# A row-wise nanmax on one core: eighteen trial operations at the start, and one load cut into nine parts by partitions and columns

## The chip, the cores and the metric

The kernel runs on one core of one Trainium2 chip. Its time is device microseconds for one launch. Times of a kernel are given as the median of its timed runs; a profile is one further execution of the same program with the hardware profiler on.

## What is computed

```python
def setup_inputs():
    batch, seq, dim = 32, 2048, 2048
    x = np.random.randn(batch, seq, dim).astype(np.float32)
    mask = np.random.rand(batch, seq, dim) < 0.1
    x[mask] = np.nan
    return {"x": x, "axis": -1}

def reference(x, axis):
    return np.nanmax(x, axis=axis).astype(np.float32)
```

65,536 rows of 2,048 floats are read (537 MB), and one maximum per row is written (0.26 MB). A tenth of the numbers are NaN, and they must not win.

## The kernel before

**Tiles.** The rows are cut into 74 tiles, listed by hand in `TILES` and gathered in six groups. The unit of the list is a quarter of a row (Q = 512 elements). The first tile is one row for each of the 128 partitions (128 x 2048); nearly all others are seven rows (128 x 14336, 7168 KB). Towards the end the tiles have the same size or less, but their loads, pieces and reductions get smaller. An entry such as `([28], [7, 9, 12], [16, 12])` says: one load of 28 quarters; three pieces of 7, 9 and 12 quarters (128 x 3584, 128 x 4608 and 128 x 6144) that are cleaned one after the other; and two reductions of 16 and 12 quarters (four rows and three rows).

**What is done with a tile.** SyncE (SP) issues the load into one of three buffers `xt0`, `xt1`, `xt2` (tile number n goes to buffer (n-1) mod 3). ScalarE (ACT) then reads the upper 16 bits of each number, with a step of two 16-bit elements, and writes a contiguous 16-bit key into one of three key buffers `kt` (through `act`, line 226 of the profile). GpSimd (POOL) turns the key back (times -1, plus a constant) and writes it over the upper half of the number, again with a step of two (through `pool`, line 236): this is the "write-back", after which a NaN counts as a very low number. A minus sign in a tile's list of pieces gives that write-back to ACT instead (`release`, also line 226). VectorE (DVE) then takes the maximum along each row with a `tensor_reduce` (line 243). At the end the rows that held nothing but NaN are mended (lines 249 and 263) and the results are stored (line 455).

**What sets the order.** All of it stands in one critical section, and the class `Order` keeps the books: each engine's instructions run in the order in which they were added, every instruction raises its engine's semaphore, and `add` puts waits in front of an instruction for those dependences that its engine has not yet seen. Loads are issued on SP at line 307, in order. Each waits for `before`, the last reduction of the tile that used the buffer three tiles ago, and for `lanes[turn]`, the load that used the same one of 14 load semaphores before it. `free[...]` holds what the next user of a buffer waits for. A key operation waits for those loads of its tile that overlap its columns (`here`), and for the write-backs that still read the key buffer.

**What the change touches.** The block of loads (line 307 and the loop around it), the setup just before the loop over tiles (after line 269), and the end of a tile's turn, where `free` is set. Tile number 30 is an ordinary one, with the entry quoted above, in buffer `xt2`.

Of the kernel before, what the change touches and what calls it, by code (L numbers as in the profile page):

```python
# [8 lines left out]
D = 2048  # L9
# [53 lines left out]
LEAD = 128  # L63

LANES = 14

# [104 lines left out]
def kernel(  # L173
# [15 lines left out]
    nc = tc.nc  # L189
    P = nc.NUM_PARTITIONS  # L190
    f32, i32 = mybir.dt.float32, mybir.dt.int32
    i16, u16 = mybir.dt.int16, mybir.dt.uint16
    ALU = mybir.AluOpType
    ACT = mybir.ActivationFunctionType
# [7 lines left out]
    of = out.bitcast(i32).flatten_outer_dims().rearrange("r c -> (r c)")  # L202
# [10 lines left out]
    xts = [sing.tile([P, WIDE * D], i32, name=f"xt{i}") for i in range(BUFS)]  # L213
# [5 lines left out]
    with tc.tile_critical():  # L219
        order = Order(nc)  # L220

        def act(deps, pair=None, **kw):
            return order.add(
                "act",
                nc.scalar,
                lambda: nc.scalar.activation(**kw),  # L226
                deps,
                lane=pair,
                joint=pair is not None,
            )  # L230

        def pool(deps, pair=None, **kw):
            return order.add(
                "pool",
                nc.gpsimd,
                lambda: nc.gpsimd.tensor_scalar(**kw),  # L236
                deps,
                lane=pair,
                joint=pair is not None,
            )  # L240

        def dve(deps, do, **kw):
            return order.add("dve", nc.vector, lambda: do(**kw), deps)  # L243

        def find(who, engine, deps, acc, none, op):
            e = order.add(
                who,
                engine,
                lambda: engine.tensor_scalar(  # L249
                    out=none,  # L250
                    in0=acc,
                    scalar1=NONE,
                    scalar2=float(0x00800000),
                    op0=ALU.is_equal,
                    op1=ALU.mult,
                ),
                deps,
            )
            bits = acc.bitcast(i32)
            return order.add(  # L260
                who,
                engine,
                lambda: engine.tensor_tensor(  # L263
                    out=bits, in0=bits, in1=none, op=op
                ),
                [e],
            )

        e_top = order.add("dve", nc.vector, lambda: nc.vector.memset(top, EDGE), [])  # L269
        act([e_top], out=warm, in_=top, func=ACT.Prelu, alpha=0.5)  # L270

        free = [[] for _ in range(BUFS)]
        kfree = [[] for _ in range(NKEYS)]
        clock = 0
# [7 lines left out]
        number = 0  # L282
        lanes = [[] for _ in range(LANES)]
        turn = 0
# [4 lines left out]
        for gi, (s, g) in enumerate(zip(rows, GROUPS)):  # L289
            xg = xr[r0 : r0 + P * s].rearrange("(p s) d -> p (s d)", p=P)  # L290
# [4 lines left out]
            base = 0  # L295
            for loads, pieces, reds in g:
                assert sum(loads) == total(pieces) == sum(reds)
                xt, before = xts[number % BUFS], free[number % BUFS]
                number += 1
                landed = []  # L300
                at = 0
                for c in loads:
                    c *= Q
                    e = order.add(
                        "sp",
                        nc.sync,
                        lambda: nc.sync.dma_start(  # L307
                            out=xt[:, at : at + c], in_=xg[:, base + at : base + at + c]
                        ),
                        before + lanes[turn],  # L310
                        lane=f"load{turn}",
                        step=16,
                    )
                    lanes[turn] = [e]
                    turn = (turn + 1) % LANES
                    landed.append((at, at + c, e))
                    at += c
                clean = []
                after = []
                at = done = 0  # L320
# [7 lines left out]
                half = {}  # L328
# [16 lines left out]
                def name(i):  # L345
                    return f"pair{number}_{pairs[i][0]}" if i in pairs else None
# [15 lines left out]
                for parts in pieces:  # L362
                    parts = parts if isinstance(parts, tuple) else (parts,)
                    c = int(sum(map(abs, parts))) * Q
                    here = [l for a, b, l in landed if a < at + c and b > at]
                    kold = []
                    if used + c > KEYS:
# [9 lines left out]
                        out=kts[key][:, used : used + c],  # L377
                        in_=xt[:, at : at + c].bitcast(i16)[:, 1::2],
                        func=ACT.Prelu,
                        bias=top,  # L380
                        scale=-1.0,
# [3 lines left out]
                    for c in parts:  # L385
                        back, wait, c = c < 0, isinstance(c, float), int(abs(c)) * Q
                        kp = kts[key][:, used : used + c]
                        used += c
                        to = xt[:, at : at + c].bitcast(i16)[:, 1::2]
# [5 lines left out]
                        else:  # L395
                            e = pool(
                                [e_key],
                                name(piece),
                                out=to,
                                in0=kp,  # L400
                                scalar1=-1.0,
                                scalar2=float(TOP),
                                op0=ALU.mult,
                                op1=ALU.add,
# [4 lines left out]
                        while reds and done + reds[0] <= min([at] + open_):  # L409
                            n = reds.pop(0)  # L410
# [5 lines left out]
                            if done % D:  # L416
                                m, to = 1, xt[:, done - 1 : done].bitcast(f32)
                            else:
                                m = max(n // D, 1)
                                to = acc[:, row : row + m]  # L420
                            e = dve(
                                [e for a, b, e in clean if b > lo and a < done] + part,
                                nc.vector.tensor_reduce,
                                out=to,
                                in_=xt[:, lo:done]
                                .bitcast(f32)
                                .rearrange("p (c d) -> p c d", c=m),
                                axis=mybir.AxisListType.X,
                                op=ALU.max,
                            )  # L430
                            part = [e] if done % D else []
                            after.append(e)
                free[(number - 1) % BUFS] = after[-1:]
                base += at
            stores.append((og, acc.bitcast(i32)))
            if gi == LATE:
# [6 lines left out]
            else:  # L443
                e = find(
                    "dve", nc.vector, after, accs[:, lo:flagged], nones[:, lo:flagged], ALU.bitwise_or
                )
                ready += [e] * (gi + 1 - len(ready))
            if gi == len(GROUPS) - 1:
                e = find("pool", nc.gpsimd, late_after, late_acc, late, ALU.add)
                ready[LATE] = e  # L450
        for (og, bits), e in zip(stores, ready):
# [5 lines left out]
                lane="store",  # L457
                step=16,
# [39 lines left out]
```

## Time and profile before

| | us |
|---|---|
| median of 2 runs | 1252.91 (1252.86 and 1252.96) |
| span of the profiled execution, first to last instruction | 1251.3 |
| what lies around the span, median less span | 1.6 |
| POOL busy | 1169.5 (93%) |
| DVE busy | 1110.9 (89%) |
| ACT busy | 986.8 (79%) |

The profiled execution has no separate device time beside its span, so 1251.3 us plus the 1.6 us around it stand for it. Line numbers with an L are lines of the kernel before; "SPq" is SP's queue of DMA issues; "xt<-kt" names output and input. In the timeline the first number is the start in us, the second the time from the first to the last of the merged instructions, and what stands in brackets is the idle time before it and what ended it. In the table by form, "busy us, mean ns" are followed by the engine's idle time before such instructions.

### The profile page before, as it was taken

To read this page: it belongs to the slowest core of one execution; us is meant where nothing else is said; L and a number is where in the kernel's file an instruction comes from. 1 tells how busy PE (TensorE), PEld (TensorE's weight loads), DVE (VectorE), ACT (ScalarE), POOL (GpSimd) and SP (SyncE) were. 2 spreads that over 40 slices of the span, in tenths; PEclk is the share of its full clock that TensorE was granted. 3 is DMA by queue.
4 is the path that set the end of the run, shared out by engine and by line. 5 is a ranking of instruction groups with operands and counts; after the bars stand their busy time and mean duration, and the time that the engine had idled before them with its cause. 6 is when DMAs were issued, how large, how long until landed. Compare 5 with 4: busy or idle time off the path is not lost.

```text
span 1251.3 us, 893 instructions
## 1 busy us (share of the span) xinstructions
DVE 1110.9 (89%) x181; ACT 986.8 (79%) x273; POOL 1169.5 (93%) x242
## 2 busy tenths in 40 slices
DVE  0888989888889888898988888998888899999999
ACT  3777887778787877788777878777777878999998
POOL 2999989998999899998999899999999999989998
DMA  9999999999999999999999999999999999999997
GB/s 415 440 412 438 440 440 438 413 440 440 440 434 416 440 440 438 434 418 440 440 438 434 418 440 440 438 434 418 440 440 437 437 418 437 436 429 431 428 429 294
DMA packets 15991, 537.20 MB, mean 429 GB/s; under 512 B 2544, under 2 KB 2544, under 8 KB 3568
## 3 DMA queue, kind: packets, MB, share of 16 engines
q1 hardware_dynamic: 15984, 537.14, 99.3%
q14 instruction: 7, 0.06, 0.0%
HBM read 536.87 MB, written 0.26 MB: 429 GB/s over the span
## 4 chain that ended last, share of the span: by engine, by line
DMA 38%; DVE 27%; POOL 20%; ACT 13%; issue 1%; SPq 0%; ACTq 0%
DMA xt<-in_x_dram 38%; DVE acc L243 27%; POOL xt L236 20%; ACT kt L226 11%; ACT xt L226 2%; SPq L307 0%; DVE none L249 0%; DVE acc L263 0%; SPq L493 0%; ACTq L158 0%; SPq L219 0%
## 5 line engine op out<-in xcount | busy, mean ns | idle before, releaser
L236 POOL TENSOR_SCALAR xt<-kt 128x3584 int16<-128x3584 uint16 (+11 forms) x236 | 1168.4, 4951 | 77.0 <-ACT kt L226 59.2
L243 DVE TENSOR_REDUCE acc<-xt 128x3 f32<-128x6144 f32 (+4 forms) x175 | 1107.6, 6380 | 136.7 <-POOL xt L236 128.8
L226 ACT ACTIVATE kt<-xt,scalars 128x3584 uint16<-128x3584 int16 (+9 forms) x247 | 935.5, 3826 | 257.4 <-DMA xt<-in_x_dram 241.1
L226 ACT ACTIVATE xt<-kt 128x512 int16<-128x512 uint16 (+6 forms) x24 | 52.8, 2202 | 0.7
L226 ACT ACT_TABLE_LOAD x1 | 1.3, 1283 | 0.9 <-SPq L219 0.9
L243 DVE TENSOR_REDUCE xt<-xt 128x1 f32<-128x1536 f32 x1 | 1.7, 1742 | 0.0
L269 DVE MEMSET scalars<- 128x1 f32 x1 | 0.1, 59 | 1.0 <-SPq L219 1.0
L249 DVE TENSOR_SCALAR none<-acc 128x414 int32<-128x414 f32 (+1 forms) x2 | 0.8, 381 | 0.1
L263 DVE TENSOR_TENSOR acc<-acc,none 128x414 int32<-128x414 int32 (+1 forms) x2 | 0.8, 375 | 0.1
L249 POOL TENSOR_SCALAR late<-acc 128x91 int32<-128x91 f32 x1 | 0.5, 547 | 0.1
L263 POOL TENSOR_TENSOR acc<-acc,late 128x91 int32<-128x91 int32 x1 | 0.3, 339 | 0.1
L479 POOL MEMSET const-float32-0.0<- 128x1 f32 x1 | 0.1, 99 | 0.2 <-issue 0.2
L226 ACT ACTIVATE scalars<-scalars 128x1 f32<-128x1 f32 x1 | 0.2, 202 | 0.0
L479 POOL MEMSET const-uint8-127<- 128x1 uint8 x1 | 0.1, 103 | 0.0
L479 POOL MEMSET const-bfloat16-1.0<- 128x1 bf16 x1 | 0.1, 102 | 0.0
L479 POOL MEMSET const-float32-1.0<- 128x1 f32 x1 | 0.1, 99 | 0.0
## 6 DMA issues: line engine op xcount, KB each, us to landing
xt<-in_x_dram SPq DMA_DIRECT2D x61, 7168.0 KB, 22.5
xt<-in_x_dram SPq DMA_DIRECT2D x2, 5120.0 KB, 17.4
xt<-in_x_dram SPq DMA_DIRECT2D x3, 2816.0 KB, 22.6
xt<-in_x_dram SPq DMA_DIRECT2D x4, 2048.0 KB, 22.2
xt<-in_x_dram SPq DMA_DIRECT2D x5, 1536.0 KB, 29.0
xt<-in_x_dram SPq DMA_DIRECT2D x2, 3584.0 KB, 24.7
xt<-in_x_dram SPq DMA_DIRECT2D x6, 1024.0 KB, 26.6
xt<-in_x_dram SPq DMA_DIRECT2D x3, 1792.0 KB, 29.9
```

Source lines behind the costliest of these rows:

```text
L226: lambda: nc.scalar.activation(**kw),
L236: lambda: nc.gpsimd.tensor_scalar(**kw),
L243: return order.add("dve", nc.vector, lambda: do(**kw), deps)
L249: lambda: engine.tensor_scalar(out=none, in0=acc, scalar1=NONE, scalar2=float(0x00800000), op0=ALU.is_equal, op1=ALU.mult,),
L263: lambda: engine.tensor_tensor(out=bits, in0=bits, in1=none, op=op),
L269: e_top = order.add("dve", nc.vector, lambda: nc.vector.memset(top, EDGE), [])
L479: nc = _bacc.Bacc("TRN2", target_bir_lowering=False, num_devices=1)
```

## The change

Two things are added, and nothing is taken out.

At the start, DVE clears 1,536 elements of 32 bits in the unused part of buffer `xt0` (the first tile fills only 2,048 of its 14,336 columns). After the first tile's work has been added, a new function `spare` adds six operations on each of POOL, ACT and DVE. Each reads 1,024 16-bit values of the cleared region and writes 1,024 16-bit values (times -1, plus 1) elsewhere in the unused part, in six forms: contiguous to every second element, contiguous to contiguous, every second to contiguous, every second to every second, and two with transposed walks (512 x 2 and 32 x 32). On each engine each waits for the one before it. The next load into `xt0`, that of tile 4, waits for the ends of all three chains as well as for the first tile's reduction. Nothing reads what the trials write.

The load of tile 30 becomes nine loads. Four blocks of columns (1,024, 1,152, 1,280 and 1,408 wide) are each cut in two at a partition (8, 120, 64 and 16), and the remaining 9,472 columns are one load over all partitions. Each part takes its own load semaphore, and the semaphores of all later loads move on by eight places. ACT's first key operation of tile 30 (columns 0 to 3,583) now waits for the first eight parts, and its second for the ninth.

```diff
+LEFT = D
+SOME = 1024
+SPLIT = 30
+BLOCKS = ((1024, 8), (1152, 120), (1280, 64), (1408, 16))
...
+        zeros = xts[0][:, LEFT : LEFT + SOME // 2 + SOME]
+        e_zero = order.add("dve", nc.vector, lambda: nc.vector.memset(zeros, 0), [])
+
+        def spare(room):
+
+            half = SOME // 2
+            of = room[:, 0:half].bitcast(i16)
+            apart = room[:, half : half + SOME].bitcast(i16)[:, 1::2]
+            e = e_zero
+            ends = []
+            at = half + SOME
+
+            def place():
+                nonlocal at
+                at += SOME
+                return room[:, at - SOME : at].bitcast(i16)
+
+            def turns(v, j):
+                return v.rearrange("p (j i) -> p i j", j=j)
+
+            for who, engine in (("pool", nc.gpsimd), ("act", nc.scalar), ("dve", nc.vector)):
+                to = place()
+                far, near = to[:, 1::2], to[:, 0:SOME]
+                forms = [(far, of), (near, of), (near, apart), (far, apart)]
+                forms += [(turns(far, j), turns(of, j)) for j in (2, 32)]
+                d = [e]
+                for o, i in forms:
+                    if who == "act":
+                        d = [act(d, out=o, in_=i, func=ACT.Copy, bias=1.0, scale=-1.0)]
+                        continue
+                    d = [
+                        order.add(
+                            who,
+                            engine,
+                            lambda: engine.tensor_scalar(
+                                out=o, in0=i, scalar1=-1.0, scalar2=1.0, op0=ALU.mult, op1=ALU.add
+                            ),
+                            d,
+                        )
+                    ]
+                ends += d
+            return ends
...
                 for c in loads:
                     c *= Q
-                    e = order.add(
...
+                    runs = [(at, at + c, 0, P)]
+                    if number == SPLIT:
+                        runs = []
+                        a = at
+                        for n, p in BLOCKS:
+                            runs += [(a, a + n, 0, p), (a, a + n, p, P)]
+                            a += n
+                        runs += [(a, at + c, 0, P)]
+                    for a, b, p, q in runs:
+                        e = order.add(
+                            "sp",
+                            nc.sync,
+                            lambda: nc.sync.dma_start(
+                                out=xt[p:q, a:b], in_=xg[p:q, base + a : base + b]
+                            ),
+                            before + lanes[turn],
+                            lane=f"load{turn}",
+                            step=16,
+                        )
+                        lanes[turn] = [e]
+                        turn = (turn + 1) % LANES
+                        landed.append((a, b, e))
                     at += c
...
                 free[(number - 1) % BUFS] = after[-1:]
+                if number == 1:
+                    free[0] = free[0] + spare(xt[:, LEFT:])
                 base += at
```

More of the change, by code (lines that the diff above doesn't have):

```diff
@@ L303 @@
                     c *= Q
-                    e = order.add(
[L305 to L316, printed above, removed]
+                    runs = [(at, at + c, 0, P)]
[20 more added lines that the diff above has]
+                        landed.append((a, b, e))
                     at += c
```

## The prediction, as it was put on record

> **What bounds the kernel now.** I read the page first (busy shares, slices, queues), then the chain that ended last, then the timeline at the two places that the change touches, then the table by form for prices.
>
> ```profile
> DVE 1110.9 (89%) x181; ACT 986.8 (79%) x273; POOL 1169.5 (93%) x242
> ...
> DMA  9999999999999999999999999999999999999997
> GB/s 415 440 412 438 440 440 438 413 440 440 440 434 416 440 440 438 434 418 440 440 438 434 418 440 440 438 434 418 440 440 437 437 418 437 436 429 431 428 429 294
> ...
> q1 hardware_dynamic: 15984, 537.14, 99.3%
> ...
> DMA 38%; DVE 27%; POOL 20%; ACT 13%; issue 1%; SPq 0%; ACTq 0%
> ```
>
> The DMA row is full in 39 of 40 slices and the load queue is busy for 99.3% of the span: the stream of loads is the bound. The chain gives DMA only 38% because it walks from a landing through ACT, POOL and DVE to the issue of the load three tiles on; that load then queues behind another, so the compute in the chain is not what sets the pace. Two stretches of the timeline show how much room there is. The first is the start:
>
> ```profile
> 0.94 50.23 SPq L307 DMA_DIRECT2D xt<-in_x_dram  x5
> 1.00 0.06 DVE L269 MEMSET scalars<- 128x1 f32 x1 [1.00 <-SPq L219]
> ...
> 5.80 2.00 ACT L226 ACTIVATE kt<-xt,scalars 128x2048 uint16<-128x2048 int16 x1 [3.42 <-DMA xt<-in_x_dram]
> 7.89 2.46 POOL L236 TENSOR_SCALAR xt<-kt 128x2048 int16<-128x2048 uint16 x1 [7.46 <-ACT kt L226]
> 10.39 2.29 DVE L243 TENSOR_REDUCE acc<-xt 128x1 f32<-128x2048 f32 x1 [9.33 <-POOL xt L236]
> 22.67 7.31 ACT L226 ACTIVATE kt<-xt,scalars 128x3584 uint16<-128x3584 int16 x2 [14.87 <-DMA xt<-in_x_dram]
> 26.04 33.68 POOL L236 TENSOR_SCALAR xt<-kt 128x3584 int16<-128x3584 uint16 x6 [15.68 <-ACT kt L226]
> ...
> 35.66 15.15 DVE L243 TENSOR_REDUCE acc<-xt 128x4 f32<-128x8192 f32 x2 [22.99 <-POOL xt L236]
> ```
>
> After the first tile ACT is idle for 14.87 us, POOL for 15.68 and DVE for 22.99, while the second load comes in. The second is tile 30, whose load lands at 496.8:
>
> ```profile
> 474.36 50.97 SPq L307 DMA_DIRECT2D xt<-in_x_dram  x4
> 476.06 15.15 DVE L243 TENSOR_REDUCE acc<-xt 128x4 f32<-128x8192 f32 x2 [1.73 <-POOL xt L236]
> 479.92 7.31 ACT L226 ACTIVATE kt<-xt,scalars 128x3584 uint16<-128x3584 int16 x2 [3.88 <-DMA xt<-in_x_dram]
> 487.53 5.42 ACT L226 ACTIVATE kt<-xt,scalars 128x6144 uint16<-128x6144 int16 x1 [0.30 <-POOL xt L236]
> 492.95 15.15 DVE L243 TENSOR_REDUCE acc<-xt 128x4 f32<-128x8192 f32 x2 [1.74 <-POOL xt L236]
> 496.81 7.31 ACT L226 ACTIVATE kt<-xt,scalars 128x3584 uint16<-128x3584 int16 x2 [3.87 <-DMA xt<-in_x_dram]
> ```
>
> Landings come 16.9 us apart (479.9, 496.8), and tile 30's load is issued at 474.36, 5.5 us before the load ahead of it lands: the queue always holds something. 7168 KB (7,340,032 B) in 16.9 us is 434 GB/s, a sixteenth of it 27.1 GB/s. POOL runs without a break here, so a tile costs it almost a load's time as well; ACT and DVE have 3.9 and 1.7 us to spare in each tile.
>
> **The trials.** Prices come from the table by form:
>
> ```profile
> L243 DVE TENSOR_REDUCE acc<-xt 128x1 f32<-128x2048 f32 x29 | 64.3, 2277 | 9.3 <-POOL xt L236 9.3
> L236 POOL TENSOR_SCALAR xt<-kt 128x1024 int16<-128x1024 uint16 x6 | 8.0, 1337 | 0.5
> L226 ACT ACTIVATE xt<-kt 128x1024 int16<-128x1024 uint16 x5 | 6.7, 1340 | 0.1
> L243 DVE TENSOR_REDUCE acc<-xt 128x1 f32<-128x513 f32 x1 | 0.7, 687 | 0.0
> ```
>
> POOL and ACT already do the first form (contiguous in, every second out), at 1,337 and 1,340 ns for 1,024 elements. The other five are not in the trace. DVE has only reductions: from 513 to 2,048 elements 1.04 ns an element, so 1.22 us for 1,024, and for clearing 1,536 elements at most 0.16 + 1.6 = 1.8 us, in DVE's idle time before 10.39.
> POOL: ends tile 1 at 10.35; 6 x 1.34 = 8.0; done at 18.4; wanted again at 26.04. ACT: ends at 7.80; 6 x 1.34 = 8.0; done at 15.9; wanted at 22.67. DVE: ends at 12.68; 6 x 1.22 = 7.3; done at 20.0; wanted at 35.66. All of it lies under the second load: cost 0. If that cover were too short, there is more. Load 5 is issued at 50.84 and load 4 lands 43.8 us after 12.7, at 56.5, so a POOL or ACT that is late by up to 5.6 us only uses up the queue's lead.
> The load of tile 4 moves from 12.70 to about 20.1 on SP. It must reach the engines before load 3 lands, at 39.6; load 1 took 4.8 us to land, of which its 1 MB is 2.4, so 37 is early enough. Cost 0. Queued behind it on SP is only load 5, at 50.84.
> The trials' ends: from below, they cannot gain, since nothing on the path is removed. From above, take each innermost run of the transposed walks as an instruction of its own, at the 99 ns that the smallest POOL operation (a 128x1 memset) takes: 512 x 0.099 + 32 x 0.099 + 4 x 1.34 = 59 us, 38 us more than 15.7 + 5.6. I take the price by elements, because POOL's rows lie on one line (1,337 ns at 1,024, 4,201 at 3,584: 1.12 ns an element plus 0.19).
> [...]
>
> **The nine parts.** The bytes are the same. SP issues nine times in place of once. At 1171.49 and on, the chain shows issues that follow each other at 0.37 to 0.48 us, so the ninth leaves by 474.36 + 8 x 0.47 = 478.1, before the load ahead has landed (479.9); and the first eight parts hold 2,432 KB, 5.7 us of the stream. The queue doesn't run dry: issues cost 0. Semaphores: each lane's earlier load landed long ago.
> ACT gets seven more waits before its first key of tile 30. At the 0.07 to 0.08 us that the chain shows as issue gaps this is 0.6 us, in an idle time of 3.87; and these parts land some 11 us before the ninth, so the first key runs in that idle time. POOL is busy with tile 29 until 500.0, so its start does not move: no gain, no cost.
> What is left is the stream itself, where a delay goes into the end one for one. Per load: by the landing records of the trace, 7168, 1024, 512 and 256 KB take 16.90, 2.44, 1.24 and 0.64 us, which is 2.354 ns a KB plus 0.03 us. Eight more: **+0.24 us**.
> Shape: all 105 loads of the trace have 128 partitions, one packet to a row, eight rows to each sixteenth. None has fewer. Lower end: the parts spread over the sixteenths in proportion, 0. Upper end: every part on one sixteenth, 2,490,368 B at 27.1 GB/s = 92 us in place of 5.7, +86. Between them: eight rows to a sixteenth, each part counted from the first, so that this one carries 16 rows of each block in place of 8: 155,648 B = 5.7 us. I take the case nearest the rows that exist, an even spread, with one exception: eight rows cannot be split evenly sixteen ways, and where the two parts of 8 partitions give one row each to half of them, these carry 4,096 + 4,608 B too many: **+0.32 us**. Shares that lag stay behind (the spread of one load's sixteen landings grows from 0.4 to 1.3 us through the run, and falls back by no more than 0.1), so this is not won back.
> [...]
>
> **Sum:** 0 + 0 + 0.24 + 0.32 = +0.6 us on 1251.3 + 1.6 = 1252.9, which is also the median of the two runs: **1253.5**.
>
> **Rivals.**
> *Parts pile up on few sixteenths* (slower). If a count such as 120 cannot be spread, its two parts, 120 x (4,096 + 4,608) = 1,044,480 B, go through one: 38.5 us less the even share of 2.4, +36: 1289. It passes 2% (25 us) when one sixteenth gets 680 KB too many. For it: no load in the trace has such a shape. Against: only that 128-partition loads spread evenly.
> *Counting from the first.* +5.7 + 0.2: 1258.8, within 2%. For it: an equal eight rows a share is what the trace shows.
> *A trial form is slow.* POOL's six would have to take over 15.7 + 5.6 = 21.3 us before anything is lost, and 46 for 2%; at the upper end 59 us give 1252.9 + 38 + 0.6 = 1291. Against: the line by elements.
> *The early key gains.* If tile 30's first key let POOL start sooner: POOL's wait there is under 0.2 us, so 1252.7 at best.
>
> **How the numbers follow.** Forecast 0.85, counting from the first 0.07, pile-up 0.04, slow trial 0.03, early gain 0.01. Range: three steps of 0.4 us in the landings (17.4, 17.3 and 17.3 us in place of 16.9, near 260, 395 and 954) belong to no instruction and may be absent or doubled: 1252.9 - 1.2 = 1251.7 below; above, the case of counting from the first, 1258.8. That holds the forecast and that rival. 2% is about what a measurement of this kernel can tell from no change. Faster 0.01, same 0.92, slower 0.07.
>
> **What would show it.** Trials: POOL's sixth ends near 18.4 and its first work on tile 2 still starts at 26.0; an end after 26 breaks the price by elements, one after 31.7 costs time. Load 4 is issued near 20. Parts: nine issues from 474.4 to 478.1; load 30 lands at 497.4 in place of 496.8, and all later landings are 0.6 late; 502 would be counting from the first, 533 the pile-up. Load 31 issued after load 30 has landed would break the claim that the queue never runs dry.

## The result, and the profile after

| | us |
|---|---|
| before, median of 2 runs | 1252.91 (1252.86 and 1252.96) |
| changed, median of 2 runs | 1264.80 (1264.45 and 1265.14) |
| ratio, with 95% interval | 1.0094 (1.0078 to 1.0110) |
| span of the profiled execution, before and changed | 1251.3 and 1263.2 |

The change costs 11.9 us, 0.9%. That is within 2% and above the range on record (1251.7 to 1258.8), which had 1253.5 as its value. In another set of runs, with 13 of the kernel before, the changed kernel took 1264.57 us against 1252.78, ratio 1.0094 (1.0079 to 1.0109).

The page of the changed kernel (its line numbers are five higher for the lines of ACT, POOL and DVE, and 57 higher for the loads, now L364):

```profile
DVE 1134.3 (90%) x188; ACT 1000.7 (79%) x279; POOL 1188.0 (94%) x248
...
GB/s 411 407 434 421 436 432 431 436 434 432 434 436 434 436 436 318 439 434 436 434 436 432 432 436 430 434 430 432 434 436 434 436 432 423 432 435 431 427 429 289
...
L311 DVE TENSOR_SCALAR xt<-xt 128x1024 int16<-128x1024 int16 x6 | 22.2, 3702 | 0.2
L311 POOL TENSOR_SCALAR xt<-xt 128x1024 int16<-128x1024 int16 x6 | 15.5, 2576 | 0.5
L231 ACT ACTIVATE xt<-xt 128x1024 int16<-128x1024 int16 x6 | 14.4, 2402 | 0.2
```

Two things stand out. The trials (L311, and the last line for ACT) took 22.2, 15.5 and 14.4 us where the forecast had 7.3, 8.0 and 8.0. And one slice in the GB/s row, the sixteenth (474 to 505 us), fell to 318: there lie the parts of tile 30.

Where the stream lost time is read from the landings of the loads, 16.9 us apart where nothing is wrong. Set against the kernel before, load 5 is 1.8 us late, load 7 4.2, load 28 3.7, load 29 5.6 and load 30 11.7; from there to the end it stays between 11.6 and 11.9. So the loss has two places, the start (about 4 us) and tile 30 (about 8).

The start, in the timeline of the changed kernel:

```profile
0.93 54.86 SPq L364 DMA_DIRECT2D xt<-in_x_dram  x5
...
7.82 14.57 ACT L231 ACTIVATE xt<-xt 128x1024 int16<-128x1024 int16 x6
...
10.55 15.87 POOL L311 TENSOR_SCALAR xt<-xt 128x1024 int16<-128x1024 int16 x6
12.71 22.38 DVE L311 TENSOR_SCALAR xt<-xt 128x1024 int16<-128x1024 int16 x6
22.77 7.31 ACT L231 ACTIVATE kt<-xt,scalars 128x3584 uint16<-128x3584 int16 x2 [0.38 <-DMA xt<-in_x_dram]
26.50 37.74 POOL L241 TENSOR_SCALAR xt<-kt 128x3584 int16<-128x3584 uint16 x6
32.79 5.42 ACT L231 ACTIVATE kt<-xt,scalars 128x6144 uint16<-128x6144 int16 x1 [2.71 <-POOL xt L241]
...
40.29 15.15 DVE L248 TENSOR_REDUCE acc<-xt 128x4 f32<-128x8192 f32 x2 [5.20 <-POOL xt L241]
```

ACT and POOL only just fit under the second load: ACT ends its trials at 22.39 with 0.38 us to spare. POOL ends its own at 26.42 and starts tile 2 at 26.50, 0.36 us after the 26.14 at which the key would have let it (ACT's start at 22.77, and the 3.37 us from there to POOL's start in the kernel before). Yet POOL's first six write-backs now take 37.74 us in place of 33.68, and DVE's first reduction of tile 2 starts at 40.29 in place of 35.66, 4.6 us late. Load 5 then leaves at 55.47 in place of 50.84; it is the last of the five issues in the first line, which end at 55.79. Load 4 waited for DVE's last trial: it left at 35.18, where the forecast had 20.1. That was still 4.5 us before load 3 landed, and it landed on time.

Tile 30, in the same view:

```profile
477.91 76.01 SPq L364 DMA_DIRECT2D xt<-in_x_dram  x13
479.70 15.15 DVE L248 TENSOR_REDUCE acc<-xt 128x4 f32<-128x8192 f32 x2 [1.81 <-POOL xt L241]
485.55 7.31 ACT L231 ACTIVATE kt<-xt,scalars 128x3584 uint16<-128x3584 int16 x2 [5.85 <-DMA xt<-in_x_dram]
...
508.59 9.44 ACT L231 ACTIVATE kt<-xt,scalars 128x4608 uint16<-128x4608 int16 x2 [6.86 <-DMA xt<-in_x_dram]
512.81 12.43 POOL L241 TENSOR_SCALAR xt<-kt 128x4608 int16<-128x4608 uint16 x2 [2.87 <-ACT kt L231]
...
525.41 7.31 ACT L231 ACTIVATE kt<-xt,scalars 128x3584 uint16<-128x3584 int16 x2 [7.38 <-DMA xt<-in_x_dram]
```

The nine issues start at 477.91. Load 29 lands at 485.5, load 30's last part at 508.5, load 31 at 525.4: 23.0 and then 16.9 us. The table by stretches of the same kernel (length, busy time of the engines with counts, clock, DMA share, GB/s) shows it as a rate:

```profile
464.00:480.00 16.00, 14.19 (x3) 12.72 (x3) 15.61 (x4) 1.00 1.03 444
481.00:497.00 16.00, 13.85 (x2) 11.17 (x3) 13.81 (x3) 1.00 1.04 230
497.00:507.00 10.00, 8.44 (x1) 4.73 (x2) 9.80 (x3) 1.00 1.04 452
```

While the parts move, the DMA engines are as busy as ever (share 1.04), but they move 230 GB/s. Busy and full are not the same; the DMA row of tenths could not have shown this, and the GB/s beside it does.

### The profile page after: what moved, and what is told of

It reads as the page before. It is cut to its first block, busy times and chain, and to the rows that moved or that the text cites. A ratio compares the mean times of both kernels' runs of the same rounds, so it can differ in the third digit from the quotient of the medians.

```text
span 1263.2 us, 926 instructions
## 1 busy us (share of the span) xinstructions
DVE 1134.3 (90%) x188; ACT 1000.7 (79%) x279; POOL 1188.0 (94%) x248
## 4 chain that ended last, share of the span: by engine, by line
DMA 34%; DVE 26%; POOL 25%; ACT 14%; issue 1%; SPq 0%; ACTq 0%
DMA xt<-in_x_dram 34%; DVE acc L248 26%; POOL xt L241 23%; ACT kt L231 13%; ACT xt L231 2%; POOL xt L311 1%; SPq L364 0%; DVE none L254 0%; DVE acc L268 0%; SPq L552 0%; ACTq L163 0%; SPq L224 0%
## 5 line engine op out<-in xcount | busy, mean ns | idle before, releaser
L311 DVE TENSOR_SCALAR xt<-xt 128x1024 int16<-128x1024 int16 x6 | 22.2, 3702 | 0.2
L311 POOL TENSOR_SCALAR xt<-xt 128x1024 int16<-128x1024 int16 x6 | 15.5, 2576 | 0.5
L231 ACT ACTIVATE xt<-xt 128x1024 int16<-128x1024 int16 x6 | 14.4, 2402 | 0.2
```

Of the source, the lines that this page charges most:

```text
L311: lambda: engine.tensor_scalar(out=o, in0=i, scalar1=-1.0, scalar2=1.0, op0=ALU.mult, op1=ALU.add),
```

## The experiments

Two theories for each place. *The start*: that DVE and POOL shut each other out (lock), against plain slow forms; and what a late load costs. *Tile 30*: that a load of fewer than 128 partitions is slow, and why, against short rows or unequal shares. Where an expectation says that tile 30 is one load, `SPLIT = 0` is set as in the first run; where it says that there are no trials, their call is left out as in the second. These lines are not printed again.

**The two halves of the change, alone.** `trials_only` sets the number of the split tile to one that does not exist, `parts_only` leaves out the call of the trials.

```diff
-SPLIT = 30
+SPLIT = 0
```

> The eighteen trials are kept, tile 30 is one load again. Lock theory (DVE's and POOL's 16-bit operations shut each other out, so that DVE's last two trials hold up POOL's first two write-backs of tile 2 by 4.4 us, the load of tile 5 leaves 4.6 us late and costs 1.7 us): 1252.9 + 1.7 = 1254.6 us, load 5 landing near 75.2. If the sixteenth that fell 2.5 us behind in load 7 of the changed kernel belongs to the trials too: 1257.1, with the same step near 110 us. Rival, the trials cost nothing and everything is the parts: 1252.9.

Measured: 1256.11 us against 1252.79, ratio 1.0027 (1.0018 to 1.0037), **+3.3**. Load 5 lands at 74.9 after a gap of 18.5, load 7 at 110.9 after one of 19.1. Both steps of the changed kernel are back, so both belong to the trials.

```diff
-                if number == 1:
-                    free[0] = free[0] + spare(xt[:, LEFT:])
```

> The nine parts of tile 30 are kept, the trials are left out. The parts' landings in the changed kernel lie 8.1 us more behind after load 30 than before load 29. If that is the parts' own cost: 1252.9 + 8.1 = 1261.0 us. Rival, the parts only bring out a lag that the start made: 1253.5.

Measured: 1259.62 us, ratio 1.0055 (1.0042 to 1.0067), **+6.8**; load 30 ends 22.8 us after load 29. The parts cost by themselves. Alone the two come to 10.1 us, together to 11.9; the rest is not accounted for (below).

**Cut by columns only.** No trials, and each block one load over all partitions.

```diff
-                            runs += [(a, a + n, 0, p), (a, a + n, p, P)]
+                            runs += [(a, a + n, 0, P)]
```

> No trials; tile 30 in five loads of 128 partitions, cut at the same columns (1024, 1152, 1280, 1408 and the rest). Theory of partitions (a load of fewer than 128 partitions runs at about half rate, whatever its rows): 1252.9 + 4 x 0.03 = 1253.0 us, packets of 4,096 B near 159 ns as in the tail of the kernel before. Rival, short rows or the number of loads in mid-stream cost it: rows of the same 4 to 5.6 KB, so 4 to 8 us more, 1257 to 1261, packets near 300 ns.

Measured: 1253.43 us, ratio 1.0005 (0.9996 to 1.0014), not to be told from no change. Loads 29 and 30 land 17.0 us apart:

```profile
480.09 7.31 ACT L231 ACTIVATE kt<-xt,scalars 128x3584 uint16<-128x3584 int16 x2 [3.90 <-DMA xt<-in_x_dram]
487.69 8.59 ACT L231 ACTIVATE kt<-xt,scalars 128x6144 uint16<-128x6144 int16 x2 [0.29 <-POOL xt L241]
497.19 4.13 ACT L231 ACTIVATE kt<-xt,scalars 128x4608 uint16<-128x4608 int16 x1 [0.91 <-DMA xt<-in_x_dram]
```

The brackets show the early key as well: the first key of tile 30 ran at the end of the group at 487.69, ahead of the landing at 497.1, and only the second had to wait. By the packet records (medians) a row of 4,096 B took 159 ns here and 281 in `parts_only`, one of 5,632 B 215 and 400. The rows are the same; the cut by partitions is what nearly doubled their time.

**Which partitions.** Tile 30 in two halves, and in three pieces around the middle, each of full width.

```diff
-                        for n, p in BLOCKS:
...
+                        runs = [(at, at + c, 0, 64), (at, at + c, 64, P)]
```

> No trials; tile 30 in two loads of its full width, partitions 0 to 63 and 64 to 127. The landings of the nine parts show equal shares at half speed (4,096 B in 281 ns in place of 159). Half-rate theory: both halves at half rate, 16.9 us each in place of 8.45: 1252.8 + 16.9 = 1269.7 us, rows of 57,344 B near 4.2 us in place of 2.1. Rival, unequal shares (64 rows split evenly sixteen ways): 1252.8 + 0.03, rows at 2.1 us.

Measured: 1273.17 us against 1252.88, ratio 1.0160 (1.0145 to 1.0176), **+20.3**. Rows of 57,344 B took 4.3 to 4.5 us in place of 2.1. Unequal shares are out: eight rows at 4.4 us make the 35.2 us that tile 30 took, so each sixteenth had its eight rows, and all are slow. In the timeline, the landings of loads 29, 30 and 31:

```profile
482.45 7.31 ACT L231 ACTIVATE kt<-xt,scalars 128x3584 uint16<-128x3584 int16 x2 [5.95 <-DMA xt<-in_x_dram]
...
517.68 7.31 ACT L231 ACTIVATE kt<-xt,scalars 128x3584 uint16<-128x3584 int16 x2 [22.22 <-DMA xt<-in_x_dram]
...
534.33 7.31 ACT L231 ACTIVATE kt<-xt,scalars 128x3584 uint16<-128x3584 int16 x2 [3.64 <-DMA xt<-in_x_dram]
```

35.2 us for tile 30 and 16.7 for the next. The half rate by itself had been expected to cost 16.9 us, 3.4 less than was measured: tile 30 took 1.4 us more than twice 16.9, and load 29, ahead of the halves and over all partitions, landed 2.1 us late. Why load 29 suffers was not tried. The three pieces:

```diff
...
+                        runs = [(at, at + c, 0, 32), (at, at + c, 32, 96), (at, at + c, 96, P)]
```

> No trials; tile 30 in three loads of its full width, partitions 0 to 31, 32 to 95 and 96 to 127. If a load of fewer than 128 partitions runs at half rate whichever they are: as the two halves, 1269.7 us. [...]

Measured: 1264.67 us, ratio 1.0094 (1.0078 to 1.0109), **+11.8**. That is 5.0 us below the 1269.7 of half rate whichever the partitions are. The pieces landed 8.5, 9.6 and 9.4 us apart: 32 partitions took as long as 64. With the middle at full rate and the outer two at half, each piece takes 8.45 us, an estimate from the 16.9 us of a whole load: 25.4 us in all, 8.45 more than the whole. Here too the loss is 3.3 us above the estimate; load 29 landed 1.9 us late, and the pieces took 27.4 us in place of 25.4. The stretches in which each piece is under way (short ones, so the rate of packets that start in them is rough):

```profile
481.00:487.00 6.00, 6.00 (x2) 5.37 (x2) 3.97 (x2) 1.00 0.78 162
490.00:496.00 6.00, 2.38 (x2) 4.65 (x1) 5.87 (x2) 1.00 1.07 459
499.00:505.00 6.00, 6.00 (x2) 0.00 (x0) 2.74 (x1) 1.00 0.87 182
```

Partitions 32 to 95 ran at full rate, with rows of 2,116 ns; 0 to 31 and 96 to 127 at half, with most rows at 4.0 to 4.7 us. So loads of 64 partitions differed by which ones they had: 2.1 us a row for 32 to 95, 4.3 to 4.5 for 0 to 63 and 64 to 127 in `halves`. Why these partitions and not those no run shows. Nor do these two runs explain the parts of 120 and 112 partitions, whose rows were slow as well (in the changed kernel, of the block cut at 120 every row of 4,608 B took 296 ns or more, of the block cut at 16 every row of 5,632 B 306 or more, where a row of 5,632 B took 215 in `columns_only`); no run has such a part alone.

**Which trials are late, and why.** First, all six forms without the transposed walks:

```diff
-                forms += [(turns(far, j), turns(of, j)) for j in (2, 32)]
```

> Tile 30 is one load; of the six trial forms on each engine the two transposed walks are left out. Both theories of the start (the walks are slow; DVE and POOL shut each other out) say that POOL is done near 16.1 us and DVE near 16.6, and that nothing is late: 1252.9 us, POOL's first work on tile 2 at 26.0. If four forms still cost over 0.5 us, it is not the walks.

Measured: 1253.06 us, ratio 1.0003 (0.9994 to 1.0012), POOL's first work on tile 2 at 25.9. The walks are needed for the loss. Then the walks taken from DVE alone:

```diff
+                if who == "dve":
+                    forms = forms[:4]
```

> Tile 30 is one load; POOL and ACT keep all six trials, DVE only the four without a transposed walk. Lock theory: POOL's walks end near 26.2 us, nothing shuts it out afterwards, its write-backs of tile 2 take 4.2 and 5.3 us as before, load 5 leaves near 51.0: 1252.8 to 1253.0. Rival, POOL's and ACT's slow walks are what is late: load 5 leaves near 55, 1256.1 as with all trials.

Measured: 1252.97 us, ratio 1.0000 (0.9991 to 1.0010). POOL and ACT do all their slow walks and nothing is lost:

```profile
10.41 15.88 POOL L313 TENSOR_SCALAR xt<-xt 128x1024 int16<-128x1024 int16 x6
12.57 9.05 DVE L313 TENSOR_SCALAR xt<-xt 128x1024 int16<-128x1024 int16 x4
...
26.37 37.88 POOL L241 TENSOR_SCALAR xt<-kt 128x3584 int16<-128x3584 uint16 x7
26.39 25.11 SPq L366 DMA_DIRECT2D xt<-in_x_dram  x2
```

POOL begins tile 2 at 26.37, as late as in the changed kernel, but load 5 leaves at 51.2. So it is DVE's last two operations that hold POOL up. DVE with nothing beside it:

```diff
-            for who, engine in (("pool", nc.gpsimd), ("act", nc.scalar), ("dve", nc.vector)):
+            for who, engine in (("dve", nc.vector),):
```

> Tile 30 is one load; only DVE has its six trials, POOL and ACT have none. Lock theory: what the six take in the changed kernel (0.90, 1.14, 1.71, 5.20, 6.93 and 6.34 us) is mostly waiting for POOL; each from the end of POOL's operation ahead of it takes about 0.6, 0.3, 0.55, 0.6, 2.3 and 2.3, so alone they take about 6.7 us and end near 19.5; 1252.9 us. Rival, DVE's forms are that slow by themselves: 22 us again, the end near 35.

Measured (one run): 1253.03 us, and the six take 8.0 us:

```profile
12.52 7.98 DVE L311 TENSOR_SCALAR xt<-xt 128x1024 int16<-128x1024 int16 x6
20.52 0.33 SPq L364 DMA_DIRECT2D xt<-in_x_dram  x1
```

The table of the changed kernel had 22.2 us for the same six: two thirds of it was waiting that the profile counts as busy. Single operations from the changed kernel's timeline show for what:

```profile
16.06 5.08 POOL L311 TENSOR_SCALAR xt<-xt 128x1024 int16<-128x1024 int16 x1
16.56 5.20 DVE L311 TENSOR_SCALAR xt<-xt 128x1024 int16<-128x1024 int16 x1
...
21.22 5.20 POOL L311 TENSOR_SCALAR xt<-xt 128x1024 int16<-128x1024 int16 x1
21.79 6.93 DVE L311 TENSOR_SCALAR xt<-xt 128x1024 int16<-128x1024 int16 x1
26.50 6.25 POOL L241 TENSOR_SCALAR xt<-kt 128x3584 int16<-128x3584 uint16 x1
```

DVE's operation at 16.56 is "busy" for 5.20 us and alone takes 0.73; it ends 0.6 us after POOL's. The next starts at 21.79, just behind POOL's last walk, and ends at 28.72, 2.3 us after it. POOL's write-back started at 26.50 and took 6.25 in place of 4.19, to 32.75: 4.0 after DVE let go. DVE's last was waiting by then, and POOL's second write-back waited for that. In this stretch the two engines took turns, an instruction each; what makes them do so no view shows.

**What a late load costs.** The trials are replaced by POOL operations of the write-back's own form, of different total length, and no other engine is touched.

```diff
...
+            for n in (3584, 3584, 3584, 3584, 2816):
+                d = [
+                    order.add(
+                        "pool",
+                        nc.gpsimd,
+                        lambda: nc.gpsimd.tensor_scalar(
+                            out=room[:, 1792 : 1792 + n].bitcast(i16)[:, 1::2],
+                            in0=room[:, 0 : n // 2].bitcast(i16),
...
```

> Tile 30 is one load; the trials are replaced by POOL operations of the write-back's own form (four of 3,584 and one of 2,816 elements, about 20.1 us from 10.35), so that POOL starts tile 2 near 30.5 in place of 26.0 and load 5 leaves near 55.3, with no other engine touched. If a load that leaves 1.1 us ahead of the landing before it costs 1.7 us and then a sixteenth that falls some 2 us behind two loads later, whatever made it late: the same 1256.1 us and the same two steps in the landings. Rival, the second step belongs to the trials: 1254.5, one step.

Measured: 1256.69 us against 1252.88, ratio 1.0029 (1.0017 to 1.0041), **+3.8**. Load 5 left at 55.67, 0.8 us ahead of load 4's landing; gaps of 18.8 at load 5 and 18.8 at load 7. The lateness does it, whatever its cause.

```profile
10.47 20.35 POOL L288 TENSOR_SCALAR xt<-xt 128x3584 int16<-128x3584 int16 x5
...
30.85 25.15 SPq L346 DMA_DIRECT2D xt<-in_x_dram  x2
30.90 33.61 POOL L241 TENSOR_SCALAR xt<-kt 128x3584 int16<-128x3584 uint16 x6
```

The same with a shorter last operation:

```diff
-            for n in (3584, 3584, 3584, 3584, 2816):
+            for n in (3584, 3584, 3584, 3584, 512):
```

> As the run with POOL kept busy, but for 17.9 us (four operations of 3,584 and one of 512 elements): POOL starts tile 2 near 28.4, load 5 leaves near 53.1, 3.4 us before load 4 lands. Theory: a load costs nothing if it leaves at least 2.9 us before the landing ahead of it (in the changed kernel 2.93 us cost nothing, 1.11 us cost 1.7): 1252.9 us, no step at load 5 or 7. Rival, any lateness puts the sixteenths out of step: a step at load 7, 1254 to 1255.

Measured: 1253.70 us against 1252.78, ratio 1.0007 (0.9998 to 1.0017), so the time alone shows no loss. The gap at load 5 was 17.9, not 16.9, with no step at load 7. The theory missed by a microsecond: 3.5 us of lead is not quite enough.

And with one more:

```diff
-            for n in (3584, 3584, 3584, 3584, 2816):
+            for n in (3584, 3584, 3584, 3584, 3584, 3072):
```

> As before, but POOL is kept busy for 25 us: it starts tile 2 near 35.5, load 5 leaves near 60.1, 3.6 us after load 4 has landed. If a load needs 2.9 us of lead: 3.6 + 2.9 = 6.5 us at load 5, and with the second step of some 2 us two loads later 1252.9 + 8.5 = 1261.4. By the working on record, which counted the whole 5.6 us of lead as free: 9.3 - 5.6 = 3.7, 1256.6.

Measured: 1261.25 us, ratio 1.0065 (1.0050 to 1.0080), **+8.5**, with gaps of 23.4 at load 5 and 18.8 at load 7. Load 5 left 3.6 us after load 4 had landed and lost 6.5, so an estimate of the time from an issue to its flow is 2.9 us.

Last, a load made late in mid-stream, with POOL held up between tiles 18 and 19:

```diff
+                if number == 18:
+                    order.add("pool", nc.gpsimd, lambda: nc.gpsimd.memset(late, 0), [])
+                    for _ in range(8):
...
```

> The kernel before, with POOL kept busy for some 5 us on a small tile of its own between tiles 18 and 19 (a memset and eight operations of 128 x 91, about 0.6 us each with their gaps), so that the load of tile 22 leaves about 0.6 us ahead of load 21's landing in place of 5.5. If a late load costs this anywhere in the stream: some 2.1 us at load 22 and some 2 us at load 24, 1256.9. Rival, the second step belongs to the start of the kernel (the first tiles or its buffers): only the first step, 1255.0.

Measured: 1254.86 us against 1252.79, ratio 1.0017 (1.0007 to 1.0026), **+2.1**. The operations were shorter than forecast:

```profile
313.87 0.18 POOL L435 MEMSET late<- 128x91 int32 x1
314.13 2.82 POOL L440 TENSOR_SCALAR late<-late 128x91 int32<-128x91 int32 x8
317.04 33.60 POOL L236 TENSOR_SCALAR xt<-kt 128x3584 int16<-128x3584 uint16 x6
```

POOL was 3.2 us late, load 22 left at 341.83, 2.4 us ahead of load 21's landing, and the gap was 18.9. There was no second step, but the load was not as late as meant, so this does not settle what the second step is. Thirteen of the sixteen landings of load 22 came at 360.9 to 361.9 and three at 362.8 to 363.2: a few landings that lag, as at load 7 in the other runs.

**The changed kernel again.**

> The changed kernel once more, beside the kernel before on the same chip. Trials alone cost 3.3 us and parts alone 6.8, 10.1 together; the changed kernel 11.9. If the rest is in the kernel and not in the chip: 1264.7 to 1264.9 us here too, with the same three places in the landings (loads 5, 7 and 29 to 30), and load 29 falling some 2 us behind where the parts alone make it 0.8.

Measured: 1264.57 us, ratio 1.0094 (1.0079 to 1.0109), **+11.8**: gaps of 18.6 at load 5, 18.9 at load 7, 18.7 at load 29, and 22.3 to the end of load 30.

## Why the prediction was wrong, point by point

**What bounds the kernel** was right. Every microsecond that the stream lost at load 5, 7 or 30 stayed to the end.

**"The price by elements" failed for the walks.** The first form was priced well (POOL 1.34 us, ACT 1.33; forecast 1.34). A transposed walk took 5.1 and 5.2 us on POOL and 4.8 and 4.9 on ACT, nearly four times as much. (Some 0.5 us of each on POOL is waiting: they began at 16.06 and 21.22, and DVE's operations ahead of them ended at 16.53 and 21.76.) The rows in the trace all stepped one or two elements, and a line through two sizes of one form says nothing of another form. The upper end had 51 us for the 512 x 2 walk; the truth lay far nearer the price by elements, but POOL's end moved from the forecast 18.4 to 26.4.

**"All of it lies under the second load: cost 0" failed, for each engine was priced by itself.** DVE's six take 8.0 us alone, near the forecast 7.3; beside POOL's they took 22.2. With POOL's own trials at 15.5 us the turns reached past 26, and each of DVE's last two then pushed a write-back of tile 2: POOL's first two took 6.3 and 7.4 us in place of 4.2 and 5.3.

**"Late by up to 5.6 us only uses up the queue's lead" failed outright.** Lateness of load 5 against the loss of the whole kernel: 2.1 us cost 0.9 (`late_small`, with an interval that takes in zero), 4.4 cost 3.3 (`trials_only`), 4.8 cost 3.8 (`late_pool`), 9.1 cost 8.5 (`late_big`); 3 us in mid-stream cost 2.1 (`mid_late`). All but about one microsecond is paid. The lead of 5.5 us is not slack: with 3.5 us the gap is already 17.9. It is paid in two instalments in all five profiles in which load 5 left less than 1.2 us ahead of load 4's landing: at load 5, where all sixteen landings are late, and about 2 us more at load 7, where one to four of the sixteen fall behind the rest. In these profiles loads 6 and 7 leave only 2.7 to 3.1 us ahead, about the estimated 2.9 us from issue to flow, and the three late landings of load 22 in `mid_late` came with a lead of 2.4. So the second instalment may be a used-up lead again; but load 6 lost nothing with the same lead, and why is open.

**"Issues cost 0" and "the early key: no gain, no cost" held**: nine issues in 3.9 us, and `columns_only`, which has five of them and the early key, is not to be told from before. So did the +0.03 us a load, within what can be measured.

**"An even spread" nearly held, and "at the rate of a 128-partition load" failed.** The rate is the step that cost most (6.8 of the 11.9 us by `parts_only`). The working took the nearest rows, all of 128 partitions, and added 0.32 us for uneven shares. In the three profiles with the nine parts one of the sixteen landings of the last part came 2.1 to 2.7 us ahead of the other fifteen, so one sixteenth had less to carry; no run shows the 0.32 us apart from the rest. But the rate was half: eight parts with 2,432 KB at 230 GB/s in place of 434 are 10.8 us in place of 5.7, and load 29's last rows were slowed as well (2.0 us in the changed kernel, 0.8 in `parts_only`).

**The rivals.** Counting from the first gave 1258.8, near the 1259.62 of `parts_only` by chance: it gives some sixteenths twice the rows at the usual time for each, but in `parts_only` the rows themselves took 281 ns in place of 159, and in `halves` the shares were equal. No part fell on one sixteenth. A slow trial was a rival that lost nothing until POOL's six took over 21.3 us; they took 15.5 and the trials cost 3.3, so it came true in kind but not by its own condition, which left out DVE's turns and counted the whole lead as free. The range would have held the trials' loss alone, but not the parts'.

**Open.** The changed kernel loses 1.6 to 1.8 us more than the trials and the parts alone add up to. Load 29 falls back by 2.0 and 1.8 us in its two profiles and by 0.8 with the parts alone; that the sixteenths already behind since load 7 (spread of landings 2.3 and 2.5 us at load 28, against 0.86 with the parts alone) meet the slow parts at a worse moment would fit. It was not tried. Nor was a part of 120 or 112 partitions by itself: whether these are slow of themselves, or through the small parts beside them, is open, and `halves` and `middle` do not decide it.

## What to carry to other kernels

A lead in a queue is slack only after the time from issue to flow is taken off (here some 2.9 us, the estimate from `late_big`); make the load late on purpose to learn how much is left. Price an access pattern from rows of the same pattern (1,024 elements on POOL took 1.34 us in the first form and 5.1 in a transposed walk, some 0.5 of it waiting), and a transfer from rows of the same partitions (a row of 4,096 B took 159 ns in a load of 128 and 281 in the parts). And where two engines show busy times that start in each other's and end just behind each other's, suspect that one is waiting inside its instruction (here 5.20 us, and 0.73 alone), and run it alone.

## What the runs showed of the hardware that was not expected

- Loads of partitions 0 to 63, 64 to 127, 0 to 31 and 96 to 127 moved at about half rate in `halves` and `middle` (most rows of 57,344 B in 4.0 to 4.7 us in place of 2.1), one of partitions 32 to 95 at full rate (2.1 us).
- Forms of one 16-bit operation on 1,024 elements: contiguous in and out 1.04 us on POOL and 1.06 on ACT, every second element out 1.34 and 1.33, transposed walks 5.1 and 5.2 (some 0.5 us of each waiting for DVE) and 4.8 and 4.9. On DVE alone 0.43, 0.73, and 2.5 to 2.7.
- The steps of 0.4 us in the landings of the kernel before go with the instruction queue: single packets of 8,192 B on q14 at 246, 255, 386, 940 and 999 us, each with one packet of the stream that starts 0.3 us later and takes 2.3 to 2.6 us in place of 2.1. That the first cause the second was not tried.
